# Four heads' values in one 512-column product, and a drain of the side queue put off to where its result is read

## The chip, the cores and the metric

The kernel runs on one core of a Trainium2 chip. The metric is device time in microseconds: the median of several executions. A hardware profile of one further execution gives the trace.

## The reference, cut to what matters

One layer of a decoder for 256 tokens, model width 2048, in float32: a combined projection, two token mixers (gated linear attention, "GLA", and dilated attention, 3 groups of 8 heads of 128), sigmoid gates, an output product and a SwiGLU.

```python
h = _rmsnorm(x, attn_norm[l])
z = h @ w_in[l]
parts = jnp.split(z, split_points, axis=-1)
q_a, k_a, v_a, g_a, lr = parts[:5]
dil_parts = parts[5:5 + n_dil]          # q, k, v of three groups, 1024 columns each
o_gla = _gla(...)
o_dil = _dilated_attention(dil_parts, rel_bias).astype(x.dtype)
merged = gate_a * (o_gla @ w_branch_gla[l]) + gate_b * (o_dil @ w_branch_dil[l])
x = x + merged @ w_out[l]
hf = _rmsnorm(x, ffn_norm[l])
gu = hf @ w_ffn_in[l]
gate, up = gu[..., :D_FF], gu[..., D_FF:]
x = x + (jax.nn.silu(gate) * up) @ w_ffn_out[l]
return _rmsnorm(x, final_norm)
```

## The kernel before, in words

Every large product is a **job** (class `Job`, made by `add`, or by `win` for columns of `w_in`). A job has a block of weight columns, up to 512 wide, and runs over all 128-row k tiles. Its weights come from memory in transfers of up to 1 MB (`dma`, line 172, three buffers `raw`). Each transfer is cut into **subs** of 1024 weight columns in all: two k tiles of a 512-column job, four k tiles of a 256-column job. For each sub ScalarE writes a rounded copy `wh` (line 121 records it), VectorE the remainder `wl` (line 184), four subs ahead of the product; five buffers of each are in turn (`split`). TensorE then makes three products for one exact one: high by high, high by low, low by high (`mains`).

There are three kinds of job. Kind "T" (line 234) holds 128 tokens of the activations as the stationary operand and lets the weight columns move: per k tile and token half three matmuls, as wide as the job. Kind "F" (also line 234) holds weights and moves 256 tokens. Kind "G" (lines 216 and 218) holds weights too, and moves 512 and 256 columns in turn.

The main loop at the end of the program goes through all subs of all jobs in order. For each sub it issues the next split, the evacuation of the job that has just ended (`pending.evac`), the hook that the job has at this sub (`pre`), a step of the side queue, the matmuls of the sub (`mains`), and another step of the side queue:

```python
sub = subs[i]
next_split()
...
    pending.evac(pending)
...
hook = sub["job"].pre.get(sub["idx"])
if hook:
    hook()
advance()
mains(sub)
advance()
```

The **side queue** (`queue`, `push`, `advance`) holds generators, first in first out: GLA heads (`gla_head`), the bias table, dilated heads (`dil_head`, 15 steps each), and transposes of a finished block (`turn_block`, line 694: three idle steps, then eight transposes into `psa`, then in its last step the split of the result on ScalarE and VectorE). `drain(tag)` runs the queue's steps without anything in between until no generator with that tag is left.

The dilated stage has four rounds r of two heads each. In a round, each of the three groups g has a "G" job for q, a "G" job for k (`evac_qk`, whose `fold` takes two copies on ScalarE and three operations on VectorE), and a "T" job of 256 columns for the values of two heads (`evac_vd`, two copies on ScalarE). The evacuation of the last pushes the two heads of the round, tag D0 to D3. The first sub of round r drains D(r-2). The results lie in blocks `z` with ten slots; `SL` gives five slots to a round.

The feed-forward stage has 11 pairs of jobs (`pair`: gate, up). The evacuation of an up job (line 792, `sg`) pushes a `turn_block` with tag A, whose result `aT[p]` is the activation of a down product. `down(p0, n, last)` makes four jobs of 4n k tiles, which read `aT[p0]` to `aT[p0+n-1]`, four k tiles of each in turn. They come after pairs 4, 8 and 10: `down(0, 4)`, `down(4, 4)`, `down(8, 3)`. In the first of the four jobs, the hook at sub 0 drains A.

Of the kernel before, what the change touches and what calls it, by code (L numbers as in the profile page):

```python
# [12 lines left out]
AF = mybir.ActivationFunctionType  # L13
# [3 lines left out]
P = 128  # L17
D = 2048
# [7 lines left out]
C_Q, C_K, C_V, C_G, C_LR, C_DIL = 0, 1024, 2048, 4096, 6144, 6160  # L26
# [34 lines left out]
def trunk_layer(ctx: ExitStack, tc: tile.TileContext, x, attn_norm, w_in, w_gk_up, b_gk, gla_norm,  # L61
# [18 lines left out]
    def ps_a():  # L80
        return psum.tile([P, 1024], F32, name="psa", tag="psa", bufs=1)

    def ps_b():
        return psum.tile([P, 512], F32, name="psb", tag="psb", bufs=2)
# [9 lines left out]
    def block(tag, i, dt=F32):  # L94
        return blk.tile([P, 1024], dt, name=f"{tag}{i}", tag=f"{tag}{i}", bufs=1)
# [17 lines left out]
    def need(func):  # L113
        if SETS[func] != table[0]:
            table[0] = SETS[func]
            nc.scalar.preload_act_table_set(table[0])

    def act(o, i, func, **kw):
        if func in SETS:
            need(func)  # L120
        nc.scalar.activation(o, i, func, **kw)  # L121
# [118 lines left out]
    def advance(n=1):  # L240
        for _ in range(n):
            if not queue:
                return
            try:
                next(queue[0][1])
                queue[0][2] ^= 1
            except StopIteration:
                queue.popleft()
                return

    def idle(n):

        for _ in range(2 * n + 1):
            yield

    def push(tag, gen):
        queue.append([tag, gen, 0])

    def drain(tag):
        while any(t == tag for t, _, _ in queue):  # L260
            advance()
# [48 lines left out]
    env = {}  # L310
# [20 lines left out]
    def view(key, slot, a, fresh=True):  # L331

        if key not in env:
            env[key] = block("z", slot).rearrange("p (a t) -> p a t", a=a)
        return env[key]
# [33 lines left out]
    def evac_t(key, slot, then=None):  # L369
        def go(job):  # L370
            v = view(key, slot, 2)
            for a in range(2):
                act(v[:, a], job.acc[a], AF.Copy, scale=env["rstd"][:, a:a + 1])
            if then:
                then()
        return go
# [137 lines left out]
    def open_dil():  # L514
        drain("bias")
        drain("B")
        gctx.close()
        env["dp"] = dctx.enter_context(tc.tile_pool(name="dtmp", bufs=1))
        load_bias(0)
        for i in range(2):  # L520
            odil.append(HiLo([env["dp"].tile([P, 1024], F32R, name=f"od{i}{j}") for j in range(2)]))

    def load_bias(h):
        if h > 7:
            return
        t = env["T", h] = env["dp"].tile([P, 3, 256], F32, name="T", tag="T", bufs=2)
        f = ftab[:, :]
        nc.scalar.dma_start(t, bass.AP(tensor=f.tensor, offset=f.offset + h * 1152,
                                       ap=[[1, P], [384, 3], [1, 256]]))
# [8 lines left out]
    def dil_head(h, r):  # L538
        dp = env["dp"]
        T = env["T", h]  # L540
        load_bias(h + 1)
        hh = h % 2
        qk = [env["qk", r, g].rearrange("p (w a) t -> p w a t", w=2)[:, :, hh] for g in range(3)]
        vv = [env["vd", r, g // 2][:, (g % 2) * 2:(g % 2) * 2 + 2, hh * P:(hh + 1) * P] for g in range(3)]
        sc = P ** -0.5
        yield
        p1 = ps_a()
        for g in range(3):
            nc.tensor.matmul(p1[:, g * 256:(g + 1) * 256], qk[g][:, 0, 128:256], qk[g][:, 1],  # L549
                             start=g != 1, stop=True, skip_group_check=True)  # L550
        yield
        s1 = dp.tile([P, 3, 256], F32, name="s1", tag="s1")
        nc.vector.scalar_tensor_tensor(s1, p1[:, :768].rearrange("p (g k) -> p g k", g=3), sc, T[:, :, ::-1],
                                       op0=ALU.mult, op1=ALU.add)
        softmax_rows(s1, 256, 3)
        yield
        p0 = ps_b()
        for g in range(3):
            nc.tensor.matmul(p0[:, g * P:(g + 1) * P], qk[g][:, 0, 0:128], qk[g][:, 1, 0:128],  # L559
                             start=g == 0, stop=True, skip_group_check=True)  # L560
        yield
        s0 = dp.tile([P, 3, P], F32, name="s0", tag="s0")
        nc.vector.scalar_tensor_tensor(s0, p0[:, :384].rearrange("p (g k) -> p g k", g=3), sc, T[:, :, 127::-1],
                                       op0=ALU.mult, op1=ALU.add)
        softmax_rows(s0, 128, 3)
        yield from idle(1)
        pt = ps_a()[:, :768].rearrange("p (g a q) -> p g a q", g=3, a=2)
        for g in range(3):
            for a in range(2):
                nc.tensor.transpose(pt[:, g, a], s1[:, g, a * P:(a + 1) * P], ident)  # L570
        yield
        e0 = dp.tile([P, 3, S], F32R, name="e0", tag="e0")
        l0 = dp.tile([P, 3, S], F32R, name="l0", tag="s1")
        e1 = dp.tile([P, 3, P], F32, name="e1", tag="e1")
        act(e0[:, :, 128:256], pt[:, :, 0], AF.Copy)
        nc.vector.tensor_sub(l0[:, :, 128:256], pt[:, :, 0], e0[:, :, 128:256].bitcast(F32))
        nc.scalar.copy(e1, pt[:, :, 1])
        yield
        pq = ps_b()[:, :384].rearrange("p (g q) -> p g q", g=3)
        for g in range(3):  # L580
            nc.tensor.transpose(pq[:, g], s0[:, g], ident)
        yield
        act(e0[:, :, 0:128], pq, AF.Copy)
        nc.vector.tensor_sub(l0[:, :, 0:128], pq, e0[:, :, 0:128].bitcast(F32))
        vh = dp.tile([P, 3, P], F32R, name="vh", tag="s0")
        vl = dp.tile([P, 3, P], F32R, name="vl", tag="vl")
        for g in range(3):
            act(vh[:, g], vv[g][:, 0], AF.Copy)
            nc.vector.tensor_sub(vl[:, g], vv[g][:, 0], vh[:, g].bitcast(F32))
        yield from idle(1)  # L590
        po = ps_b()
        for g in range(3):
            for m, (st, mv) in enumerate(((vh, e0), (vh, l0), (vl, e0))):
                nc.tensor.matmul(po[:, 0:256], st[:, g], mv[:, g], start=g == 0 and m == 0, stop=False,  # L594
                                 skip_group_check=True)
            nc.tensor.matmul(po[:, 128:256], vv[g][:, 1], e1[:, g], start=False, stop=g == 2, skip_group_check=True)  # L596
        yield
        hl, j = odil[h // 4], h % 4
        act(hl.hi(j), po[:, :S], AF.Copy)
        nc.vector.tensor_sub(hl.lo(j), po[:, :S], hl.hi(j).bitcast(F32))  # L600

    def evac_qk(r, g, w, slot):
        def go(job):
            fold(job, view(("qk", r, g), slot, 4)[:, 2 * w:2 * w + 2], "R")
        return go

    def evac_vd(r, g, slot, then=None):
        def go(job):
            z = view(("vd", r, g // 2), slot, 4)
            for a in range(2):  # L610
                act(z[:, (g % 2) * 2 + a], job.acc[a], AF.Copy, scale=env["rstd"][:, a:a + 1])
            if then:
                then()
        return go


    h_acts = acts_of(hT)

    def win(kind, col, n, evac, pre=None):
        add(Job(kind, w_in, 0, KT, col, n, 8 if n <= 256 else 4, h_acts, evac, pre))  # L620
# [28 lines left out]
    win("T", C_V + 512, 512, evac_t(("v", 1), 1, after_b))  # L649


    SL = ((2, 3, 4, 5, 6), (7, 8, 9, 0, 1))
    for r in range(4):
        sl = SL[r % 2]
        for g in range(3):
            base = C_DIL + 3072 * g + 256 * r
            first = {}
            if g == 0:
                first = {0: lambda r=r: drain(f"D{r - 2}")}
            win("G", base, 256, evac_qk(r, g, 0, sl[g]), first)  # L660
            win("G", base + 1024, 256, evac_qk(r, g, 1, sl[g]))

            def then(r=r):
                if r == 0:
                    open_dil()
                for h in (2 * r, 2 * r + 1):
                    push(f"D{r}", dil_head(h, r))
            win("T", base + 2048, 256, evac_vd(r, g, sl[3 + g // 2], then if g == 2 else None))


    merged = []
# [145 lines left out]
    def down(p0, n, last):  # L817
        acts = lambda ki, p0=p0: (aT[p0 + ki // 4], ki % 4)
        for c in range(4):
            pre = {0: lambda: drain("A")} if c == 0 else None  # L820
            add(Job("T", w_ffn_out, p0 * 512, 4 * n, 512 * c, 512, 4, acts, evac_down(c, last), pre, pairs=fpair()))

    for p in range(11):
# [122 lines left out]
    job = jobs[-1]  # L946
# [58 lines left out]
```

## Time and profile before

| | us |
|---|---|
| median of 3 runs | 1910.02 (1909.5 to 1910.79) |
| profiled execution, its own time | 1908.82 |
| its span in the trace | 1907.1 |
| TensorE matmuls busy | 1882.8 (99%) |
| TensorE weight loads busy | 1621.7 (85%) |
| VectorE busy | 1025.5 (54%) |
| ScalarE busy | 863.6 (45%) |
| DMA read and written | 186 GB/s over the span |

The span goes from the first to the last instruction; 1.7 us of the execution lie around it. Weight loads run beside matmuls, so the two rows of TensorE don't add up. In the chain of waits each piece is what the next one had to wait for; a piece "x96" is 96 instructions that followed each other without a gap, so its length by 96 is the time from one start to the next.

### The profile page before, as it was taken

The numbers are of one execution on the slowest core, as the hardware profiler recorded it, in microseconds if no ns is written. First come the engines' busy times: TensorE is split into PE (matmuls) and PEld (weight loads), VectorE is DVE, ScalarE is ACT, GpSimd is POOL, SyncE is SP. The second block draws the span as 40 slices with busy tenths as digits, with TensorE's granted clock in tenths as the row PEclk, the third lists the DMA queues.
The fourth block names the chain that finished last, engine by engine and source line by source line (L and its number), as shares of the span: only waits on it lengthen the run. The fifth ranks groups of instructions, "written<-read, shape, count | busy, mean of one in ns | idle before, by whom it ended". The sixth has DMA issues, their size and how long they took to land.

```text
span 1907.1 us, 24024 instructions
## 1 busy us (share of the span) xinstructions
PE 1882.8 (99%) x9900; PEld 1621.7 (85%) x9900; DVE 1025.5 (54%) x1146; ACT 863.6 (45%) x1083; POOL 22.4 (1%) x35
## 2 busy tenths in 40 slices
PE   8999999999999999999999999999999999999998
PEld 8988988899999998888888888888788888788876
DVE  6446646656565655555555555445445544454544
ACT  6446545544444444534444445444433444334433
POOL 0000000000000000000000000000000000000001
PEclk9999999999999999999999999999999999999999
DMA  7655454455555565465666655555555555455543
GB/s 249 213 183 177 155 193 160 158 178 179 183 174 187 177 198 182 160 218 196 203 198 235 228 187 188 197 181 196 177 176 199 186 189 194 160 198 199 182 164 117
DMA packets 219589, 356.38 MB, mean 187 GB/s; under 512 B 6123, under 2 KB 91175, under 8 KB 219480
## 3 DMA queue, kind: packets, MB, share of 16 engines
q1 hardware_dynamic: 214480, 346.18, 53.7%
q0 software_dynamic: 1728, 5.51, 1.4%
q10 hardware_dynamic: 3272, 3.16, 0.6%
q8 instruction: 77, 1.26, 0.3%
q14 instruction: 32, 0.26, 0.0%
HBM read 352.70 MB, written 2.13 MB: 186 GB/s over the span
## 4 chain that ended last, share of the span: by engine, by line
PE 98%; DVE 1%; ACT 0%; DMA 0%; issue 0%; SPq 0%; DVEq 0%; ACTq 0%
PE acc L234 67%; PE psb L234 12%; PE acc L216 9%; PE acc L218 5%; PE psa L694 1%; PE psa L549 1%; PE psb L594 0%; PE psa L471 0%; PE psb L453 0%; PE psb L559 0%; PE psb L596 0%; PE psa L570 0%; DVE wl L184 0%; DMA o<-in_x_dram 0%; PE psa L301 0%; PE psa L234 0%
## 5 line engine op out<-in xcount | busy, mean ns | idle before, releaser
L184 DVE TENSOR_TENSOR wl<-raw,wh 128x1024 fp32r<-128x1024 f32 (+2 forms) x655 | 794.1, 1215 | 807.0 <-ACT wh L121 805.4
L121 ACT ACTIVATE wh<-raw 128x1024 fp32r<-128x1024 f32 (+2 forms) x655 | 685.5, 1049 | 884.2 <-PE acc L234 624.0
L234 PE MATMUL acc<-wh,h 128*128 128x512 f32 (+3 forms) x2880 | 791.7, 358 | 0.0
L234 PEld LDWEIGHTS acc<-wh,h 128*128 128x128 f32 x2880 | 515.4, 189 | 76.5 <-issue 1.6
L234 PE MATMUL acc<-wl,h 128*128 128x512 f32 (+3 forms) x1440 | 513.6, 357 | 0.0
L234 PEld LDWEIGHTS acc<-wl,h 128*128 128x128 f32 x1440 | 272.0, 189 | 37.0 <-DVE wl L184 0.2
L216 PE MATMUL acc<-h,wh 128*128 128x512 f32 x768 | 273.6, 400 | 0.0
L218 PE MATMUL acc<-h,wl 128*128 128x256 f32 x768 | 214.9, 280 | 0.0
L234 PE MATMUL acc<-wh,z 128*128 128x512 f32 (+1 forms) x648 | 199.5, 387 | 0.0
L216 PEld LDWEIGHTS acc<-h,wh 128*128 128x128 f32 x768 | 144.2, 188 | 35.2 <-issue 1.3
L218 PEld LDWEIGHTS acc<-h,wl 128*128 128x128 f32 x768 | 144.9, 189 | 0.2
L234 PEld LDWEIGHTS acc<-wh,z 128*128 128x128 f32 x648 | 121.5, 189 | 24.4
L234 PE MATMUL acc<-wl,z 128*128 128x512 f32 (+1 forms) x324 | 125.2, 387 | 0.0
L234 PE MATMUL psb<-wh,h 128*128 128x512 f32 x384 | 119.9, 390 | 0.0
L234 PE MATMUL psb<-wh,z 128*128 128x512 f32 x304 | 96.0, 395 | 0.0
L234 PE MATMUL acc<-h,wh 128*128 128x256 f32 x512 | 92.5, 283 | 0.0
L234 PEld LDWEIGHTS psb<-wh,h 128*128 128x128 f32 x384 | 72.1, 188 | 14.9
L234 PEld LDWEIGHTS acc<-h,wh 128*128 128x128 f32 x512 | 80.0, 192 | 0.2
L234 PE MATMUL acc<-wh,o 128*128 128x512 f32 x256 | 79.5, 389 | 0.0
L234 PE MATMUL psb<-wl,h 128*128 128x512 f32 x192 | 74.7, 389 | 0.0
L234 PE MATMUL acc<-h,wl 128*128 128x256 f32 x256 | 72.4, 283 | 0.0
L234 PEld LDWEIGHTS acc<-wl,z 128*128 128x128 f32 x324 | 61.0, 188 | 12.2
(202 smaller groups left out, 1160.9 us busy)
## 6 DMA issues: line engine op xcount, KB each, us to landing
raw<-in_w_in_dram SPq DMA_DIRECT2D x144, 1024.0 KB, 4.8
raw<-in_w_ffn_in_dram SPq DMA_DIRECT2D x88, 1024.0 KB, 4.8
raw<-in_w_ffn_out_dram SPq DMA_DIRECT2D x44, 1024.0 KB, 5.0
raw<-in_w_branch_gla_dram SPq DMA_DIRECT2D x16, 1024.0 KB, 5.0
raw<-in_w_out_dram SPq DMA_DIRECT2D x16, 1024.0 KB, 4.9
raw<-in_w_branch_dil_dram SPq DMA_DIRECT2D x8, 1024.0 KB, 4.9
raw<-in_w_in_dram SPq DMA_DIRECT2D x8, 692.0 KB, 4.0
z<-in_b_gate_dram POOLq DMA_DIRECT2D x8, 512.0 KB, 8.1
```

Source lines behind the costliest of these rows:

```text
L121: nc.scalar.activation(o, i, func, **kw)
L184: nc.vector.tensor_sub(wl[:, :k * n], src, wh[:, :k * n].bitcast(F32))
L216: nc.tensor.matmul(job.acc[j], wh[:, kk, j * P:(j + 1) * P], hl.both(aj), start=first, stop=last, skip_group_check=True)
L218: nc.tensor.matmul(job.acc[j][:, 0:S], wl[:, kk, j * P:(j + 1) * P], hi, start=False, stop=last, skip_group_check=True)
L234: nc.tensor.matmul(dst, st, mv, start=first and i == 0 and j % per_bank == 0, stop=last and i == 2, skip_group_check=True)
L549: nc.tensor.matmul(p1[:, g * 256:(g + 1) * 256], qk[g][:, 0, 128:256], qk[g][:, 1], start=g != 1, stop=True, skip_group_check=True)
L694: nc.tensor.transpose(pt[:, j * S + a * P:j * S + a * P + P], src[:, a, j * P:(j + 1) * P], ident)
```

## The change

Values: the twelve "T" jobs of 256 columns (two heads of a group) become six of 512 columns (four heads of a group), made in rounds 0 and 2 behind the round's six "G" jobs, with `evac_t`. Rounds 1 and 3 have "G" jobs alone, and the evacuation of the last one pushes the round's heads. A head reads its columns out of the block of its group and pair of rounds. Three slots hold the values of two rounds. GLA's tag B, and D1, are drained at the first sub of the second value job.

Down product: the hook that drains A moves from sub 0 of the first job to sub 2(n-1), where the first k tile of `aT[p0+n-1]` is read: sub 6, 6 and 4 of the three.

```diff
@@ dil_head
-        vv = [env["vd", r, g // 2][:, (g % 2) * 2:(g % 2) * 2 + 2, hh * P:(hh + 1) * P] for g in range(3)]
+        c = 2 * (r % 2) + hh
+        vv = [env["vd", r // 2, g][:, :, c * P:(c + 1) * P] for g in range(3)]
@@
-    def evac_vd(r, g, slot, then=None):
-        def go(job):
-            z = view(("vd", r, g // 2), slot, 4)
-            for a in range(2):
-                act(z[:, (g % 2) * 2 + a], job.acc[a], AF.Copy, scale=env["rstd"][:, a:a + 1])
-            if then:
-                then()
-        return go
@@
-    SL = ((2, 3, 4, 5, 6), (7, 8, 9, 0, 1))
+    def push_heads(r):
+        for h in (2 * r, 2 * r + 1):
+            push(f"D{r}", dil_head(h, r))
+
+    def first_heads():
+        open_dil()
+        push_heads(0)
+
     for r in range(4):
-        sl = SL[r % 2]
         for g in range(3):
             base = C_DIL + 3072 * g + 256 * r
-            first = {}
-            if g == 0:
-                first = {0: lambda r=r: drain(f"D{r - 2}")}
-            win("G", base, 256, evac_qk(r, g, 0, sl[g]), first)
-            win("G", base + 1024, 256, evac_qk(r, g, 1, sl[g]))
-
-            def then(r=r):
-                if r == 0:
-                    open_dil()
-                for h in (2 * r, 2 * r + 1):
-                    push(f"D{r}", dil_head(h, r))
-            win("T", base + 2048, 256, evac_vd(r, g, sl[3 + g // 2], then if g == 2 else None))
+            first = {0: lambda r=r: drain(f"D{r - 2}")} if g == 0 else None
+            slot = ((2, 3, 4), (8, 0, 1))[r % 2][g]
+            win("G", base, 256, evac_qk(r, g, 0, slot), first)
+            then = evac_qk(r, g, 1, slot)
+            if r % 2 and g == 2:
+                def then(job, f=then, r=r):
+                    f(job)
+                    push_heads(r)
+            win("G", base + 1024, 256, then)
+        if r % 2 == 0:
+
+            for g in range(3):
+                then = (first_heads if r == 0 else lambda: push_heads(2)) if g == 2 else None
+                first = {0: lambda r=r: drain("D1" if r else "B")} if g == 1 else None
+                win("T", C_DIL + 3072 * g + 2048 + 256 * r, 512,
+                    evac_t(("vd", r // 2, g), ((5, 6, 7), (9, 5, 6))[r // 2][g], then), first)
@@ down
-            pre = {0: lambda: drain("A")} if c == 0 else None
+            pre = {2 * (n - 1): lambda: drain("A")} if c == 0 else None
```

The order of the instructions shows what moved. On TensorE, where the last up job of pair 4 ends and `down(0, 4)` begins (`sg` is the block of the pair, `z_10151` and `z_10447` hold activations of earlier pairs), before:

```order
L234 MATMUL acc<-wh,h_9871 128x512 x2
L234 MATMUL acc<-wl,h_9871 128x512
L234 MATMUL acc<-wh,h_9871 128x512
L694 MATMUL psa<-ident,sg 128x128 x8
L234 MATMUL psb<-wh,z_10151 128x512
L234 MATMUL psb<-wl,z_10151 128x512
```

And in the change (the rows left out are further products of the first two subs):

```order
L234 MATMUL acc<-wl,h_9281 128x512
L234 MATMUL acc<-wh,h_9281 128x512
L234 MATMUL psb<-wh,z_9561 128x512
L234 MATMUL psb<-wl,z_9561 128x512
...
L234 MATMUL psb<-wl,z_9562 128x512
L234 MATMUL psb<-wh,z_9562 128x512
L696 MATMUL psa<-ident,sg 128x128 x8
L234 MATMUL psb<-wh,z_9857 128x512
```

The eight transposes stood between the up job and the down job; they now stand behind the down job's first two subs, 24 matmuls later. The same is so at `down(4, 4)` and `down(8, 3)`.

On VectorE, in round 0, at the second GLA head of tag B (`gk`, `pb`, `bl`, `kd` are its tiles; `acc,fold` is the evacuation of a "G" job), as the difference:

```order
 L184 TENSOR_TENSOR wl<-raw,wh 128x1024
 L407 SCALAR_TENSOR_TENSOR gk<-psb,ge 128x512
 L408 SCALAR_TENSOR_TENSOR pb<-inside,gk 128x512
 L184 TENSOR_TENSOR wl<-raw,wh 128x1024
+L319 TENSOR_TENSOR z_3071<-acc,fold 128x256 x2
+L321 TENSOR_TENSOR z_3071<-z_3071,R 128x512
 L421 COPY bl<-pb 128x8
 L425 SCALAR_TENSOR_TENSOR kd<-pb,bl 128x256 x2
```

The evacuation of a "G" job now stands ahead of the head's next VectorE step, where ScalarE's evacuation of a value job was.

On VectorE, from the end of the bias table (`fs`) to the first dilated head (`s`), in the change:

```order
L184 TENSOR_TENSOR wl<-raw,wh 128x1024
L319 TENSOR_TENSOR z_3327<-acc,fold 128x256 x2
L321 TENSOR_TENSOR z_3327<-z_3327,R 128x512
L509 COPY fs<-psb 8x384
L184 TENSOR_TENSOR wl<-raw,wh 128x1024 x25
L554 SCALAR_TENSOR_TENSOR s_3934<-psa,T 128x768
L533 TENSOR_REDUCE st<-s_3934 128x1
```

Before, 13 splits in three pieces, with two folds between them, lay between `fs` and `s`; now 25 splits lie there without a step of the side queue. The value jobs of round 0 stand in that place.

## Rows read from the trace of the kernel before

**Rows 1.** The page: busy time, share and instructions of each engine.

```profile
PE 1882.8 (99%) x9900; PEld 1621.7 (85%) x9900; DVE 1025.5 (54%) x1146; ACT 863.6 (45%) x1083; POOL 22.4 (1%) x35
```

**Rows 2.** The page's chain of waits, shares by engine.

```profile
PE 98%; DVE 1%; ACT 0%; DMA 0%; issue 0%; SPq 0%; DVEq 0%; ACTq 0%
```

**Rows 3.** Waits: who waited for whom, us in total, times, longest.

```profile
PE psa L694 <- DVE sg L792: 10.0, 5, 3.2
...
ACT wh L121 <- DMA raw<-in_w_in_dram: 9.3, 5, 2.4
```

**Rows 4.** Groups of instructions by form: value matmuls of 256 columns; value evacuations.

```profile
L234 PE MATMUL acc<-wh,h 128*128 128x256 f32 x768 | 142.9, 285 | 0.0
...
L121 ACT ACTIVATE z<-acc,r_attn 128x256 f32<-128x256 f32 x24 | 9.9, 463 | 0.0
...
L121 ACT ACTIVATE z<-acc,r_attn 128x512 f32<-128x512 f32 x12 | 7.5, 677 | 0.0
```

**Rows 5.** Chain of waits, dilated stage: start us, us, what. Whole value jobs.

```profile
400.06 11.52 PE acc L234 x96
...
477.02 11.51 PE acc L234 x96
...
511.14 11.52 PE acc L234 x96
```

**Rows 6.** Chain of waits: 512-column "T" matmuls beside a dilated head, and alone.

```profile
748.96 2.75 PE acc L234 x12
...
1175.26 21.76 PE psb L234 x96
```

**Rows 7.** Chain of waits at the three starts of a down product.

```profile
1374.71 1.06 ACT wh L121
...
1377.03 1.33 DVE sg L792 x2
...
1379.99 22.82 PE psb L234 x96
1402.81 43.52 PE acc L234 x192
...
1644.89 1.06 ACT wh L121
...
1672.79 43.52 PE acc L234 x192
...
1826.04 1.06 ACT wh L121
...
1848.44 16.32 PE psb L234 x72
```

**Rows 8.** Stretches: length, busy of PE, PEld, DVE, ACT, POOL, then PEclk.

```profile
1380.00:1382.40 2.40, 2.40 (x7) 1.88 (x7) 1.25 (x2) 1.09 (x2) 0.00 (x0) 0.58 0.00 0
1382.40:1402.80 20.40, 20.40 (x91) 16.86 (x90) 8.61 (x8) 7.43 (x7) 0.00 (x0) 1.00 0.47 154
```

**Rows 9.** Chain of waits where a pair is followed by another pair.

```profile
1197.02 5.44 PE acc L234 x24
1202.47 0.87 PE psa L694 x8
```

**Rows 10.** Chain of waits: last bias-table product; last products of D0.

```profile
379.34 0.74 PE psb L508 x2
...
459.80 0.36 PE psb L594 x3
```

**Rows 11.** Timeline at the second GLA head of tag B.

```profile
340.70 0.29 DVE L434 TENSOR_TENSOR sA<-kd,el 128x128 f32<-128x128 f32 x1
...
344.63 0.61 PE L453 MATMUL psb<-mA,sA 128*128 128x128 f32 x4
```

**Rows 12.** Groups of instructions: the operations of a fold on VectorE.

```profile
L319 DVE TENSOR_TENSOR z<-acc,fold 128x256 f32<-128x256 f32 x48 | 18.0, 416 | 0.0
...
L321 DVE TENSOR_TENSOR z<-z,R 128x512 f32<-128x512 f32 x24 | 16.6, 693 | 0.8
```

## The prediction

> **What bounds the kernel now.** I read the page's busy times first. TensorE's matmuls fill 99% of the span, VectorE 54%, ScalarE 45% [rows 1], and the chain that ended last is 98% TensorE [rows 2]. So a saving counts only if it takes time off TensorE, and work on the other engines counts only where TensorE waits for it. Next the waits: TensorE's one large wait is that of transposes into `psa` for VectorE's `sg` (10.0 us in all); weights that come late are felt by ScalarE alone, 9.3 us in five places [rows 3]. Then two pieces of the chain of waits: the dilated stage, for the price of a value matmul, and the starts of the down products, for the price of the drain.
>
> I count changes of 0.2% (3.8 us) and more as faster or slower, which is about what a measurement of this kernel can tell from no change.
>
> **Value jobs.** There are twelve; their 768 matmuls on `wh` [rows 4] and half as many on `wl` make 1152, 96 a job. A whole job takes 11.51 to 11.52 us without a gap [rows 5], which is 120.0 ns from one matmul to the next. A job of 512 columns of the same kind takes 21.76 us for 96 [rows 6], 226.7 ns each. Both figures fit one rule, worked out from the two: a column costs (226.7 - 120.0) / 256 = 0.417 ns, and each matmul 13.3 ns on top, whatever its width. The change keeps the columns and halves the matmuls: 12 x 11.52 = 138.2 us become 6 x 21.76 = 130.6 us. **Gain 7.7 us**, all of it on the path, since the chain runs through these matmuls.
>
> The lower bound: beside a dilated head twelve such matmuls took 2.75 us [rows 6], 229.2 ns each; at that price the gain is 576 x (240.0 - 229.2) = 6.2 us. I take the undisturbed price. In the new order the heads are pushed behind the value jobs, so they run beside "G" jobs; 25 splits with no side work stand on VectorE where the value jobs of round 0 are.
>
> The Trainium skill, "TensorE: Matmul & The Clock Gate", section "Wait — 56ns, not 53.3ns?", puts the fixed cost of a matmul at the full clock at about 2.5 ns. By that figure the 576 matmuls saved would be worth an estimated 1.4 us. The 13.3 ns of this trace differ from it, and the trace decides.
>
> **What goes with the value jobs and costs nothing.** ScalarE's evacuations fall from 24 x 463 ns to 12 x 677 ns [rows 4], 11.1 to 8.1 us; they were hidden behind TensorE and are still. Splits and transfers keep their number and size (1 MB), the transfers' rows double in length; no transfer is on the chain now [rows 2]. The "G" jobs keep their matmuls. What moves is when side work meets evacuations. At the second GLA head of tag B a fold on VectorE, 2 x 416 + 693 = 1.53 us [rows 12], now stands ahead of the head's chain. That chain ended with `sA` at 340.70 + 0.29 = 340.99, and TensorE used it at 344.63 [rows 11], so 3.6 us of slack cover 1.5 us. If such cover failed, it would cost the excess once per place, below 2 us.
>
> The drains. The bias table, last of the B work, ran its last product at 379.34 [rows 10], 85.6 us into the dilated stage (it began at about 293.7); the new drain of B comes after six "G" jobs and one value job. Two "G" jobs lie between the end of one value job (477.02 + 11.51) and the next at 511.14 [rows 5], so one takes 11.3 us, and the drain comes 6 x 11.3 + 21.8 = 89.6 us in, with the B work's own matmuls on top. By count it is safer: the B work takes 52 steps, 26 subs, and the drain is at sub 32. Round 1 has now 24 subs for D0, where it had 36. Two heads take 30 steps, 15 subs; the trace shows the last of D0 at 459.80 [rows 10], 48 us after the round began at 411.58 [rows 5], and the new round takes 67.8 us and the heads' own matmuls. So these drains find nothing to run. Cost 0.
>
> **Down products.** At the start of each, the chain leaves TensorE [rows 7]. The last matmul of the up job frees the buffer for a split (ScalarE 1.06 us from 1374.71, then VectorE), VectorE evacuates `sg` (1.33 us, from 1377.03), and only then can the drained transposes run; the products behind them start at 1379.99. The 96 matmuls of the first job then take 22.82 us and not 21.76: the granted clock was 0.58 from 1380.00 to 1382.40 and 1.00 after it [rows 8], so for a part of this stretch it was at the lower of its two levels, 1.2 GHz, after TensorE had stood idle. From 1374.71 to the next job at 1402.81 it is 28.10 us. Without the drain it is 21.76 us and 0.87 us for the eight transposes, the price where a pair follows a pair [rows 9], 22.63 together. Gain 5.47 us. The second start, 1644.89 to 1672.79 [rows 7], gives 27.90 - 22.63 = 5.27 us. The third has 72 matmuls, 16.32 us [rows 7], and runs from 1826.04 to 1848.44: 22.40 - 16.32 - 0.87 = 5.21 us. **Gain 15.95 us** in all, if the whole wait goes.
>
> Does it go? Behind sub 1 the transposes stand 24 matmuls, 5.44 us, after the up job's last. The evacuation ends at 1377.03 + 1.33 = 1378.36, 3.65 us after it [rows 7], so 1.8 us are left. The trace has this very case: a pair followed by a pair runs 24 matmuls, then the transposes, then goes on with no wait [rows 9]. What comes next is the split of the transposed block, in the side queue's step in sub 2. It is used first in another job after pairs 4 and 8, and in sub 4 of `down(8, 3)`, two subs (5.4 us) later; the split needs two copies on ScalarE and two subtractions on VectorE beside their usual 45 to 54%. The moved drains find an empty queue. The other banks of `psum` are used in the same turn as before. So nothing else is late, and the clock does not fall, for want of an idle time.
>
> **The sum.** 7.7 + 15.95 = 23.6 us off the profiled execution's 1908.82 us: 1885.2 us. The median of the runs stood 1.2 us above that execution, so the forecast for the median is **1886.4 us**, 1.2% less. With the lower bound for the values it is 1887.9 us; nothing excludes a microsecond or two more gain, since evacuations and matmuls of fewer jobs change hands less often, so 1884 us is the lower end.
>
> **Rivals.**
>
> *The values give nothing* (0.05). TensorE would spend its time per column, and a matmul's 13.3 ns would come back as a wait between "T" matmuls and "G" matmuls, or for evacuations of 512 columns. For it: 229.2 against 226.7 ns beside a head. Against it: the same kind of job, with the same evacuation, runs 96 matmuls in 21.76 us elsewhere. It gives 1910.0 - 15.95 = 1894.1 us. By the figure of the Trainium skill quoted above, which would make this rival nearly true, it would be 1.4 us less.
>
> *The wait moves with the drain* (0.05). The transposes would still come too early, or the first products on the new block would wait for its split. Most likely at `down(8, 3)`, which reads the block soonest. For it: 1.8 us of slack is little, and a split could come in between. Against it: the undisturbed pairs [rows 9]. If one of the three places keeps its wait, the time is 1886.4 + 5.2 = 1891.6 us; if all three do, 1902.4 us.
>
> *Slower: rounds 1 and 3 are too short for their heads* (0.02). If the two heads needed more than 24 subs, `drain` would run the rest step by step, and TensorE would wait for the softmax before each head's transposes and for the conversions before its last products. A drained step of this sort cost 5.2 to 5.5 us at the down products [rows 7]. Two such waits in each of the four heads of rounds 0 and 2 would cost some 42 us, an estimate from these rows, so the time would be 1928 us. It decides only from the point where 30 steps don't fit into 48; the trace and the count of steps speak against it.
>
> *The change does less than it says* (0.02): a tile's slot is still read when a value job's evacuation wants it (slots 5, 6, 7 and 9 held GLA's tensors), ScalarE stands behind that wait, and the splits come late. One such wait of a few us at each of two places: about 1890 us.
>
> **How the numbers follow.** My forecast has 0.86, the rivals 0.14. The forecast's own range is 1884 to 1888.5 us. I stretch it to 1890.5 us, to take in part of the smaller waits (one late place, a fold in the way); what lies above, the first rival and the larger part of the second, is left out at about 0.1. Faster by over 0.2%: the forecast and the first, second and fourth rival, 0.97 with something off for what I don't see. Within 0.2%: 0.02. Slower: 0.02.
>
> **What the changed profile would show.** Right: the "T" group of 256 columns on `wh,h` is gone, that of 512 columns has 384 more; a value job appears as 96 matmuls in about 21.8 us; the wait of `psa` transposes for `sg` is below 1 us; the chain runs from the up job straight into the down job at all three places, with the granted clock at 1.00; TensorE's busy time falls by 10 us or less, and the span by 23 us. Wrong: a new wait of TensorE for `wh`, `wl`, `z` or `psa`; value matmuls 230 ns apart or more; a gap in front of the ninth k tile of `down(8, 3)`.

## The result, and the profile after

The change takes 1886.51 us (median of four runs, 1885.85 to 1886.74) where the kernel before takes 1909.76 us (four runs, 1908.55 to 1910.79). The ratio is 0.9878, with a 95% interval of 0.9861 to 0.9895: 1.2% faster, against a forecast of 1886.4 us. The profiled execution took 1885.85 us, its span 1884.1 us, 23.0 us less than before.

The page of the change, busy times and chain by engine:

```profile
span 1884.1 us, 22852 instructions
...
PE 1869.7 (99%) x9324; PEld 1587.7 (84%) x9324; DVE 1025.3 (54%) x1146; ACT 861.5 (46%) x1071; POOL 22.3 (1%) x35
...
PE 98%; DVE 1%; ACT 0%; DMA 0%; issue 0%; SPq 0%; DVEq 0%; ACTq 0%
```

TensorE has 576 matmuls less and is still the bound, as in [rows 1] and [rows 2]. VectorE's work is what it was.

The groups by form, "T" matmuls of 512 columns on the projection and the feed-forward, which answer to [rows 4]:

```profile
L234 PE MATMUL acc<-wh,h 128*128 128x512 f32 x2304 | 719.6, 390 | 0.0
...
L234 PE MATMUL acc<-wl,h 128*128 128x512 f32 x1152 | 448.3, 389 | 0.0
```

The group of 256 columns on `wh,h` is gone, and that of 512 columns has 384 more, 2304 where it had 1920.

The chain of waits, value jobs of rounds 0 and 2 (start us, us, what), which answers to [rows 5]:

```profile
376.31 2.95 PE acc L234 x12
379.26 0.74 PE psb L508 x2
380.00 62.79 PE acc L234 x276
...
595.80 65.31 PE acc L234 x288
```

Round 0's 288 matmuls took 2.95 + 62.79 = 65.74 us, round 2's 65.31 us: 131.05 us where the prediction had 130.6. They are 226.8 ns apart in round 2. The last product of the bias table stands among the first of them, as the order showed.

The chain of waits at the three starts of a down product, which answers to [rows 7]:

```profile
1329.50 38.09 PE acc L234 x168
1367.60 5.44 PE psb L234 x24
1373.04 0.87 PE psa L696 x8
1373.92 16.34 PE psb L234 x72
1390.25 43.52 PE acc L234 x192
...
1632.29 5.44 PE psb L234 x24
1637.73 0.87 PE psa L696 x8
1638.61 16.34 PE psb L234 x72
...
1786.40 27.20 PE acc L234 x120
1813.60 0.87 PE psa L696 x8
```

The last 168 matmuls of the pair (72 of its gate job, 96 of its up job) run straight into the down job's first 24, the transposes take their 0.87 us, and nothing waits. At the third start the 96 of the up job and the first 24 of the down job are one piece of 120. The stretch that took 28.10 us takes 22.65. In the stretches at the three starts the granted clock (the column before DMA's share) stays at 1.00, where it was 0.58 in [rows 8]:

```profile
1367.00:1390.00 23.00, 23.00 (x107) 19.15 (x106) 12.56 (x13) 9.46 (x10) 0.00 (x0) 1.00 0.54 183
1632.00:1655.00 23.00, 23.00 (x107) 19.12 (x106) 12.33 (x12) 9.48 (x11) 0.00 (x0) 1.00 0.56 183
1808.10:1825.30 17.20, 17.20 (x82) 14.33 (x81) 9.87 (x10) 7.34 (x8) 0.00 (x0) 1.00 0.57 184
```

But there is a wait that was not there before. The waits of the weight loads (engine, what it waited for, us in total, times, longest):

```profile
PEld psa L550 <- DVE z L321: 0.9, 2, 0.5
```

And the chain at the first of the two places, the start of round 2:

```profile
521.39 0.68 DVE z L319 x2
...
522.09 0.70 DVE z L321
...
522.84 0.70 PE psa L550 x2
```

The heads of round 1 are pushed by the evacuation of the round's last "G" job, and their first product (line 550, 549 before) comes one sub later. It reads the block that this very evacuation writes: the fold's last operation, line 321, starts at 522.09 and takes 0.70 us, and the last two of the head's six matmuls start behind it at 522.84. Before, a value job stood between the last "G" job and the push, so the list of waits before has no such entry. The same happens in the chain that begins at 737.39 us, with the heads of round 3.

### The profile page after: what moved, and what is told of

It reads as the page before. It is cut to its first block, busy times and chain, and to the rows that moved or that the text cites. A ratio compares the mean times of both kernels' runs of the same rounds, so it can differ in the third digit from the quotient of the medians.

```text
span 1884.1 us, 22852 instructions
## 1 busy us (share of the span) xinstructions
PE 1869.7 (99%) x9324; PEld 1587.7 (84%) x9324; DVE 1025.3 (54%) x1146; ACT 861.5 (46%) x1071; POOL 22.3 (1%) x35
## 4 chain that ended last, share of the span: by engine, by line
PE 98%; DVE 1%; ACT 0%; DMA 0%; issue 0%; SPq 0%; DVEq 0%; ACTq 0%
PE acc L234 67%; PE psb L234 12%; PE acc L216 9%; PE acc L218 5%; PE psa L696 1%; PE psa L550 0%; PE psb L595 0%; PE psa L471 0%; PE psb L453 0%; PE psb L560 0%; PE psb L597 0%; PE psa L571 0%; DMA o<-in_x_dram 0%; PE psa L301 0%; PE psa L234 0%; PE psb L398 0%
## 5 line engine op out<-in xcount | busy, mean ns | idle before, releaser
L234 PE MATMUL acc<-wh,h 128*128 128x512 f32 (+2 forms) x2496 | 768.5, 386 | 0.0
L234 PEld LDWEIGHTS acc<-wh,h 128*128 128x128 f32 x2496 | 467.2, 188 | 91.4 <-issue 2.0
L234 PE MATMUL acc<-wl,h 128*128 128x512 f32 (+2 forms) x1248 | 479.9, 385 | 0.0
L234 PEld LDWEIGHTS acc<-wl,h 128*128 128x128 f32 x1248 | 235.0, 188 | 44.2
```

Source lines behind the costliest of these rows:

```text
L234: nc.tensor.matmul(dst, st, mv, start=first and i == 0 and j % per_bank == 0, stop=last and i == 2, skip_group_check=True)
```

## The experiments

All times below are medians. The runs come in two groups, each with the kernel before on the same chip: it took 1909.16 us (eight runs, 1907.89 to 1909.44) beside the first four kernels and 1910.03 us (seven runs, 1908.74 to 1911.29) beside the others. Ratios are to these. The change itself was run again in the second group alone. Where a run of the first group is set against its 1886.51 us, the difference is good to about 0.6 us, by which the kernel before differs between the two (1909.16 and 1909.76).

### The value jobs alone, and the drain alone

The first kernel is the change with the old drain, the second the kernel before with the new one:

```diff
@@ down, value jobs alone
-            pre = {2 * (n - 1): lambda: drain("A")} if c == 0 else None
+            pre = {0: lambda: drain("A")} if c == 0 else None
@@ down, drain alone
-            pre = {0: lambda: drain("A")} if c == 0 else None
+            pre = {2 * (n - 1): lambda: drain("A")} if c == 0 else None
```

> The change with its value jobs, and with the drain of A back at sub 0 of a down product's first job. Theory (the two parts add up): the three waits of 5.2 to 5.5 us come back, with the fallen clock behind them, so 1886.5 + 15.95 = 1902.5 us, 7.3 us less than the kernel before. Rival (the parts help each other, or most of the gain is the drain's and the values give only the 1.4 us that a fixed cost of 2.5 ns a matmul would make): within 2 us of the kernel before, 1908 to 1910 us.

> The kernel before with the moved drain alone. Theory: the three waits go, 1909.8 - 15.95 = 1893.8 us, and the chain runs from the up job into the down job. Rival (the wait moves: the transposes or the first products on the new block are late): more than 1898 us, with a wait of TensorE for sg or z at a down product.

Measured: the drain alone 1893.96 us, ratio 0.992 (0.9905 to 0.9935), as expected. The value jobs alone 1904.07 us, ratio 0.9967 (0.9953 to 0.9981), in five runs from 1900.18 to 1904.31 us. That is 1.6 us above the expectation, and 5.1 us below the kernel before where 7.3 were expected. The rival's 1908 to 1910 us is not met either, and the trace shows where most of the 1.6 us are. The chain of waits of the value jobs alone, at the three starts of a down product:

```profile
1368.53 1.06 ACT wh L121
...
1372.22 1.75 PE psa L696 x7
1373.97 23.64 PE psb L234 x96
1397.61 43.52 PE acc L234 x192
...
1639.68 1.06 ACT wh L121
...
1667.77 43.52 PE acc L234 x192
...
1821.04 1.06 ACT wh L121
...
1843.70 16.32 PE psb L234 x72
```

And the stretch behind the first wait:

```profile
1374.00:1378.00 4.00, 4.00 (x11) 3.07 (x11) 1.29 (x2) 1.08 (x2) 0.00 (x0) 0.53 0.00 0
1378.00:1397.60 19.60, 19.60 (x88) 16.20 (x87) 8.58 (x7) 7.43 (x7) 0.00 (x0) 1.00 0.51 161
```

The wait is that of [rows 7], but the clock stayed near its lower level for 4 us, where it was back after 2.4 us in [rows 8]. So the first job took 23.64 us, not 22.82. This start cost 1397.61 - 1368.53 - 22.63 = 6.45 us, where it cost 5.47 in the trace of before. The other two, worked out in the same way, cost 5.46 and 5.47 us in place of 5.27 and 5.21, so the three together took 1.4 us more. The runs differ in the same way: the run of 1900.18 us had a mean granted clock of 0.997, those around 1904 us 0.995. The gain of the value jobs alone can therefore not be read from these times to better than 2 us. The traces tell more: that of the value jobs alone has them at the very lengths of the change (62.79 and 65.31 us), and that of the drain alone takes 657.18 us from the start of the feed-forward stage to the end of the first job of `down(8, 3)`, which is the change's 657.19 (worked out further below). So each part gives alone what it gives in the change.

### The value matmuls in halves

Same jobs and same order, but twice as many matmuls:

```diff
@@ mains
+                    if getattr(job, "halves", False):
+                        for q in range(2):
+                            w = slice(q * 256, q * 256 + 256)
+                            nc.tensor.matmul(dst[:, w], st, mv[:, w], start=first and i == 0 and q == 0,
+                                             stop=last and i == 2, skip_group_check=True)
+                        continue
```

> The change, with each 512-column matmul of the six value jobs written as two of 256 columns: same jobs, transfers, splits, evacuations and order, 576 matmuls more. Theory (the gain of the values is the time that each matmul costs beside its columns, 13.3 ns): 576 x 13.3 ns = 7.7 us come back, 1894.2 us, value matmuls 120 ns apart. Rival (the gain came from what else moved: fewer evacuations, heads beside other jobs, other banks): 1886.5 to 1888 us.

Measured: 1893.54 us, 7.0 us more than the change's 1886.51; the span is 1891.7 us, 7.6 more. It is also within 0.4 us of the 1893.96 us that the drain alone took beside it. The chain of waits, round 2's value jobs:

```profile
599.65 69.11 PE acc L237 x576
```

That is 120.0 ns for each matmul of 256 columns, and 3.8 us more than the change's 65.31 in this round. So the gain of the value jobs is the number of matmuls; fewer evacuations, other neighbours and other banks are worth nothing that shows here. With 13.3 ns each, 576 matmuls make 7.7 us.

The prediction drew its rule, 0.417 ns a column and 13.3 ns a matmul, through two widths alone. The trace of the kernel before has a third, 346 columns, near its start (chain of waits, 36 to 52 us):

```profile
35.88 16.23 PE acc L234 x102
```

That is 159 ns a matmul, where the rule gives 157.5. Every matmul of these jobs has its own weight load, so the runs don't tell whether the fixed time belongs to the matmul or to its load.

The fixed 2.5 ns that the Trainium skill gives ("TensorE: Matmul & The Clock Gate", "Wait — 56ns, not 53.3ns?") would have made an estimated 1.4 us; the run does not bear it out for this kernel.

### The drain one sub later

```diff
@@ down
-            pre = {2 * (n - 1): lambda: drain("A")} if c == 0 else None
+            pre = {1: lambda: drain("A")} if c == 0 else None
```

> The change, with the drain of A at sub 1 of a down product's first job: 12 matmuls (2.72 us) stand ahead of the transposes, and their block is ready 3.65 us after the up job's last matmul. Theory (the price is what is missing to the evacuation, and the clock falls only behind the long idle time): about 0.95 us at each of three places, with the granted clock at 1.00, so 1889.4 us. Rival (draining early is what costs, however early): near 1902 us. Second rival (each wait brings the clock down, short ones too): 0.95 + 0.7 us at each, 1891.5 us.

Measured: 1889.67 us, 3.2 us more than the change. The chain of waits, the first start of a down product (it runs over the evacuation; the 12 matmuls of the down job's first sub run beside the first pieces, and the 84 are the rest of that job):

```profile
1367.89 1.07 ACT wh L121
...
1370.21 1.33 DVE sg L794 x2
...
1371.59 0.98 PE psa L696 x7
1372.57 19.07 PE psb L234 x84
1391.64 43.52 PE acc L234 x192
```

And the granted clock behind it:

```profile
1367.90:1372.50 4.60, 3.89 (x21) 2.93 (x20) 3.35 (x4) 2.11 (x2) 0.00 (x0) 1.00 0.72 228
1372.50:1375.00 2.50, 2.50 (x13) 2.04 (x12) 1.70 (x3) 1.09 (x2) 0.00 (x0) 1.00 0.32 38
```

From 1367.89 to 1391.64 it is 23.75 us, 1.1 us more than the change's 22.65. TensorE stood idle for 0.7 us of it (4.60 less 3.89), and the clock did not fall. The other two starts are 1.1 us longer too, and three times 1.1 us is the whole difference. So what the drain costs is the time by which it comes ahead of the evacuation; the clock's part was paid behind the long wait, in which TensorE stood idle for 3.7 us, and not behind this one. The first rival is out by 12 us, the second by nearly 2.

### The drain at more places

```diff
@@ pair
-                    {5: lambda: drain("X")} if first else None, pairs=fpair()))
+                    {5: lambda: drain("X")} if first else {0: lambda: drain("A")} if col < FF else None,
+                    pairs=fpair()))
```

> The change, with a drain of A at sub 0 of each gate job that follows an up job: eight places where the side queue's transposes came two subs later. Theory (a drained step costs the wait for its evacuation, 4.4 to 4.6 us, and 0.6 to 1.9 us for the fallen clock behind it, each time): 8 x 5.2 to 8 x 6.4 us more, 1928 to 1938 us. Rival (the cost belongs to the start of a down product, its transfers and its other weights): less than half of that.

Measured: 1932.63 us, against 1886.43 us of the change in the same group: 46.2 us, 5.8 us for each of the eight places. The chain of waits at the first two of them:

```profile
1190.96 1.06 ACT wh L121
...
1193.27 1.33 DVE sg L794 x2
1194.65 1.75 PE psa L696 x7
1196.40 44.06 PE acc L234 x192
1240.49 1.06 ACT wh L121
...
1245.16 23.37 PE psb L234 x96
```

The same links as in [rows 7], in places that have nothing to do with a down product. So the price belongs to the drained step and not to the down product's transfers or weights. The 96 matmuls behind it took 23.37 us at the second place, where 21.76 is usual; at the first, 192 took 44.06 us where 43.52 is usual. Over the eight places the matmuls behind the wait took 0.5 to 1.9 us more than usual.

### The push a little later

The new wait, at the start of round 2 and of the gate jobs behind round 3, taken away by two subs of delay:

```diff
     def push_heads(r):
+        if r % 2:
+            push(f"D{r}", idle(1))
```

> The change, with two subs of delay ahead of the heads of rounds 1 and 3. In the change's trace their first product follows the evacuation that ends the block it reads, and TensorE stands still for about 0.5 us at each of two places. Theory (the wait is for that evacuation alone): both waits of psa for z go, and the span falls by 1.0 us, to about 1883.1 us; the time to about 1885.5 us. Rival (what is saved there comes back later in the head, or in the delayed head's last steps): the span stays at 1884.1 us.

Measured: 1885.51 us (1884.72 to 1886.33), where the change in the same group took 1886.43 us (1886.38 to 1886.86); the span is 1883.4 us, against 1884.1 in the first profile of the change and 1884.7 in its second. The wait for line 321 is gone from the list of waits, and the head's first product runs through:

```profile
527.50 1.29 PE psa L550 x6
```

The difference in time, 0.9 us, is near the limit of what can be told, but it agrees with the two waits of 0.5 us that left the trace.

### A version that is faster than both

GLA's q and k, made as "G" jobs, with the later push:

```diff
-    win("F", C_K + 512, 512, evac_zf(("k", "A"), 2))
-    win("F", C_Q + 512, 512, evac_zf(("q", "A"), 3))
+    def win_g(col, key, slot, pre=None):
+        for w in range(2):
+            def ev(job, w=w):
+                fold(job, view(key, slot, 4)[:, 2 * w:2 * w + 2], "R")
+            win("G", col + 256 * w, 256, ev, pre if w == 0 else None)
+
+    win_g(C_K + 512, ("k", "A"), 2)
+    win_g(C_Q + 512, ("q", "A"), 3)
@@
-    win("F", C_K, 512, evac_zf(("k", "B"), 8))
-    win("F", C_Q, 512, evac_zf(("q", "B"), 9), {0: lambda: drain("A")})
+    win_g(C_K, ("k", "B"), 8)
+    win_g(C_Q, ("q", "B"), 9, {0: lambda: drain("A")})
```

> As the run with the later push, and GLA's four q and k jobs of kind F (three matmuls of 256 columns, 360 ns) made as eight jobs of kind G (512 and 256 columns, 345 to 353 ns). Theory (a matmul costs its columns and 13.3 ns, wherever it stands): 256 x 10 ns = 2.6 us less, with the later push 3.6 us less than the change: 1882.9 us. Rival (the fold on VectorE beside GLA's heads makes TensorE wait): not less than the change, with a new wait in the first 300 us.

> The change itself, on the same chip as the other runs of this group, to compare them with: 1886.5 us, 1.2% less than the kernel before.

Measured: this version 1883.61 us (1883.58 to 1884.39), ratio to the kernel before 0.9863 (0.9846 to 0.9879). The change itself 1886.43 us, ratio 0.9878 (0.9863 to 0.9893). The groups of "G" matmuls of this version grow by 256 each, from 768:

```profile
L216 PE MATMUL acc<-h,wh 128*128 128x512 f32 x1024 | 365.2, 400 | 0.0
...
L218 PE MATMUL acc<-h,wl 128*128 128x256 f32 x1024 | 286.5, 280 | 0.0
```

No new wait shows in the first 300 us. The step from the later push alone is 1.9 us where 2.6 were expected, so the direction holds and the size is roughly there. Against the change it is 2.8 us, 0.15%: less than the 0.2% that the prediction counts as a difference, but in four runs each, on the same chip, that do not overlap.

## Why the prediction was right

**The sum.** It had 7.7 us for the value jobs and 15.95 us for the down products. From a job at the start of the feed-forward stage, 1175.26 [rows 6], to the end of the first job of `down(8, 3)`, 1848.44 [rows 7], it was 673.18 us; the change takes from 1168.18 to 1825.37, 657.19 us. That is 15.99 us. The rest of the 23.0 us lies ahead of the feed-forward stage. That stage begins 7.1 us earlier, although the dilated stage began 0.4 us later in the profile of the change, so the stretch between the two gave 7.5 us, where 7.7 were forecast. Here are the two rows of the change for these ends:

```profile
1168.18 21.76 PE psb L234 x96
...
1825.37 16.32 PE psb L234 x72
```

**The price of a matmul.** Right: 226.8 ns against 226.7, and the halves put it back. That the forecast of 1886.4 us comes within 0.1 us of the median is luck: the profiled execution took 1885.85 us where the sum had 1885.2, and the median stood 0.7 us above it where the prediction had added 1.2.

**The moved drains find nothing to run.** Right at the down products, and at B, D0, D1 and D2: TensorE's lists of waits have no entry for them. The fold in front of the second GLA head of tag B was absorbed too, as the slack of [rows 11] had it.

**"So nothing else is late" was not quite right.** The prediction looked at where a fold delays a head that is running and missed where it delays a head that starts. With no value job between, the push and the evacuation it depends on fell together. It cost two waits of 0.5 us. A new wait for `z` or `psa` stood in its list of signs that it was wrong; this one came, and was small. The "G" jobs gave about as much back: by the starts in the two traces, a pair of "G" matmuls without side work takes 349.8 ns on average after the change, where it took 350.8, worth some 0.8 us over 768 pairs. The drain alone, with the old value jobs, has 350.8 too, and the halves 349.6, so it goes with the order of the jobs and not with the width of the value matmuls. Why it does is open.

**"TensorE's busy time falls by 10 us or less" did not come.** It fell by 13.1 us, from 1882.8 to 1869.7. Of the 15.95 us at the down products only 11.1 were idle time. The prediction named the matmuls behind the wait as slower (by the chain 2.4 us at the three starts together), and left the drained transposes inside the stretch without a price of their own. They ran at the lower level of the clock too. Here are the stretches of the transposes at the three starts, before:

```profile
1378.40:1380.00 1.60, 1.60 (x8) 1.60 (x9) 0.00 (x0) 0.00 (x0) 0.00 (x0) 0.57 0.25 91
1648.57:1650.33 1.76, 1.76 (x8) 1.76 (x9) 0.00 (x0) 0.00 (x0) 0.00 (x0) 0.50 0.19 66
1829.73:1831.48 1.75, 1.75 (x8) 1.75 (x9) 0.00 (x0) 0.00 (x0) 0.00 (x0) 0.50 0.18 69
```

They took 5.1 us in place of three times 0.87, and so 2.5 us of busy time went with the wait. With these two and the 7.7 us of the values it makes 12.6 of the 13.1 us. The sum holds, since it was taken from whole stretches; the split into idle and busy time did not.

**The rivals.** The values gave their amount, the wait did not move with the drain (it would have been at `sg` or at `z`), rounds 1 and 3 were long enough (the drains behind them found nothing to run), and TensorE has no wait that a late evacuation of a value job would have left.

## What to carry to other kernels

Where TensorE is the bound and every matmul has its own weight load, count matmuls as well as columns: the same kind of job at two widths in a trace gives the fixed price of a matmul (here 13.3 ns), a third width checks it, and it multiplies. A drain, or any step run "now", should stand where its result is read, and there it should have at least the length of the longest chain in front of it as cover; here 12 matmuls were 1.1 us too few and 24 were enough. When a job that stood between a writer and its reader is moved away, look at the writer's tail: it was cover.

## What the runs showed that was not expected

The price of an idle time of TensorE has a second part that is not the same each time. Behind waits of one kind, the granted clock stayed near its lower level for 2.4 us in one profile and for 4 us in another, and 96 matmuls took 22.82 us [rows 7], 23.37 and 23.64 us in place of 21.76. The five runs of the value jobs alone, with three such waits, spread over 4.1 us; the four of the change, without them, over 0.9 us. But the kernel before has the same three waits, and its eight and seven runs in the two groups spread over 1.6 and 2.6 us, so the number of such waits alone does not explain the spread. What sets the length is open: no run here separates it.

The short waits of the drain one sub later, 0.7 us of idle time and 1.1 us of path at each start, left the clock at 1.00 in the stretches read at all three.
